# Weight halves by two GpSimd DMAs from the 21st chunk on, in a two-layer encoder on one core

## The chip, the core and the metric

One core of one Trainium2 chip. The time is device microseconds for one execution of the whole program, the median of the timed runs. The engines are TensorE (PE; PEld is its weight load), VectorE (DVE), ScalarE (ACT), GpSimd (POOL) and SyncE (SP); sixteen DMA engines move data between HBM and SBUF.

## The reference

512 tokens of 1024 channels, float32, two layers:

```
h = rmsnorm(x); q, k, v, x_rec, gate = split(h @ w_in)          # 1024 -> 2560
att = attention of 8 heads of 64 in a window of 8 x 16 on a 64-wide grid, with a learned bias
rec = (forward + backward gated linear recurrence of conv4(x_rec)) * gelu(gate)
x = x + concat(rmsnorm(att), rmsnorm(rec)) @ w_out              # 1024 -> 1024
u_act, u_lin = split(rmsnorm(x) @ w_up)                         # 1024 -> 2 x 3072
x = x + (gelu(conv3(u_act)) * u_lin) @ w_down                   # 3072 -> 1024
y = rmsnorm(x) after the second layer
```

## The kernel before

Channels lie on the partitions and the 512 tokens along the free axis. Each large product is done in three products of float32r halves (`mm3`): the weights' leading half with the activations' leading half, the leading half with the activations' rest, and the weights' rest with the leading half. A half of a weight block is 128 x 128, and a chunk is eight blocks, 128 x 1024, so that a chunk has 24 products of 512 columns. `weight_plan` lists the 205 chunks in the order in which TensorE takes them.

The weight stream has three steps. `load_to` has SyncE load chunk i into a buffer of `p_raw` (three buffers, 512 KB each). `split_to` has ScalarE copy it into a buffer of `p_hi` as float32r, which rounds it (line 173), and VectorE subtract that from the raw chunk into a buffer of `p_lo` (line 174); `p_hi` and `p_lo` have four buffers each. `chunk` hands chunk i to the products, and before that asks for splits up to chunk i + 3 and loads up to chunk i + 6.

Per layer the order is: the recurrence's input (4 chunks); a mixing stage in the order written out in `MIX` (queries, keys, recurrence gates, values and gate branch, with the heads' scores, softmax, transposes and products with the values in between); the output projection; the MLP, where `w_up` columns and VectorE's and ScalarE's work on a tile alternate, and `w_down` follows after each half of the hidden channels. The normalisations' scale 1/rms is applied to results later: TensorE sums squares over channels (`columns`), VectorE scales, GpSimd raises to the power -1/2 (line 319), and TensorE spreads the result over the partitions (`rows`, line 326). GpSimd otherwise only clears buffers: each layer's query tiles get 16 memsets (line 509).

The instructions of each engine run in the order that a scheduler wrote down when the program was built, from the program's order, priorities and buffers coming free. A buffer is taken again when all that used it is done; an instruction that needs one waits at the head of its engine's queue.

Of the kernel before, what the change touches and what calls it, by code (L numbers as in the profile page):

```python
# [14 lines left out]
P = 128  # L15
# [12 lines left out]
MASKED = -1e30  # L28
HALF = NJ // 2

# query blocks of 8 grid columns: first key column, number of key columns, offset of the bias
BLOCKS = [(0, 16, 0)] + [(8 * j - 8, 24, 128) for j in range(1, 7)] + [(48, 16, 320)]
NBIAS = 448
URGENT = 100000
# products that raise the tensor engine's clock while the first loads are under way
WARM = 9


# Order of the tensor engine's work between the recurrence's input and the output projection: tiles of
# queries, keys, values and the gate branch (whole, or halves a and b of the contraction), the recurrence's  # L40
# convolution c and gates t, scores S of a head, its transposed probabilities T and products with the values P, values
# by token u, the first steps of an output tile o.
MIX = ("q0 c0 c1 k0 t0 k1 q1 c2 t1 q2 k2 c3 t2 k3 q3 S0 v0a T0 t3 v0b g0a v1a S1 u0 P0 "
       "T1 g0b S2 v1b S3 g1a u1 T2 P1 v2a T3 P2 S4 S5 v2b g1b g2a T4 g2b P3 u2 P4 T5 S6 "
       "v3a v3b P5 g3a T6 S7 u3 o0 g3b P6 T7 o1 P7 o2 o3 o4 n o5 o6").split()
# [1 line left out]


def weight_plan():
    """128 x 128 weight blocks in the order in which the tensor engine takes them, eight a chunk."""  # L50
    plan = []
    for l in range(L):
        def pairs(w, k0, nk, ms):
            for k in range(k0, k0 + nk, 2):
                plan.append((w, l, [(k + a, m) for a in range(2) for m in ms]))

        def column(w, m):
            plan.append((w, l, [(k, m) for k in range(8)]))

        pairs("w_in", 0, 8, [12, 13, 14, 15])  # L60
        for step in MIX:
            if step in ("t0", "t0a", "t2", "t2a"):
                t = int(step[1])
                plan.append(("gate", l, [(t + a, dg) for a in range(2) for dg in range(4)]))
            elif step[0] in IN_TILE and step[-1] != "b":
                column("w_in", IN_TILE[step[0]] + int(step[1]))
        for m in range(0, 8, 2):
            plan.append(("w_out", l, [(a, m + b) for b in range(2) for a in range(4)]))
        pairs("w_out", 4, 4, [0, 1, 2, 3])
        for m in (4, 6):  # L70
            plan.append(("w_out", l, [(4 + a, m + b) for b in range(2) for a in range(4)]))
        for hf in range(2):
            j0 = hf * HALF
            for j in range(j0, j0 + HALF):
                if j == 0:
                    pairs("w_up", 0, 8, [0, NJ, 1, NJ + 1])
                elif j > 1:
                    column("w_up", j)
                    column("w_up", NJ + j)
            pairs("w_down", j0, HALF, [0, 1, 2, 3])  # L80
            seq = [(j0 + k, m) for m in range(4, 8) for k in range(HALF)]
            for i in range(0, len(seq), 8):
                plan.append(("w_down", l, seq[i:i + 8]))
    return plan
# [15 lines left out]
def encoder(ctx: ExitStack, tc: tile.TileContext, x_d, w_d, cols_d, bias_d, out_d):  # L100
# [15 lines left out]
    p_a = pool("p_a", 6)  # L116
    p_r = pool("p_r", 3)
    p_s = pool("p_s", 8)
    p_raw = pool("p_raw", 3)
    p_hi = pool("p_hi", 4)  # L120
    p_lo = pool("p_lo", 4)
    p_b = pool("p_b", 2)
    PS = bass.MemoryType.PSUM
# [19 lines left out]
    def urgent(level=2):  # L143
        return tc.high_priority(offset=level * URGENT) if level else ExitStack()

# [1 line left out]
    raws, halves = {}, {}  # L147
    state = {"load": 0, "split": 0, "use": 0}
    AHEAD_LOAD, AHEAD_SPLIT = 6, 3

# [3 lines left out]
    def load_to(n):  # L154
        while state["load"] < min(n, len(plan)):
            i = state["load"]
            raws[i] = p_raw.tile([P, 1024], F32, tag="raw", name=f"raw{i}")
            for n, sl in enumerate(pieces(i)):
                nc.sync.dma_start(raws[i][:, sl], w_d[i][:, sl])
                if i == n == 0:  # L160
                    nc.sync.dma_start(x[0], x_d[0])
            state["load"] += 1

    def split_to(n):
        while state["split"] < min(n, len(plan)):
            i = state["split"]
            load_to(i + 1)
            raw = raws.pop(i)
            hi = p_hi.tile([P, 1024], F32R, tag="hi", name=f"hi{i}")
            lo = p_lo.tile([P, 1024], F32R, tag="lo", name=f"lo{i}")  # L170
            with urgent(0):
                for sl in pieces(i):
                    nc.scalar.activation(hi[:, sl], raw[:, sl], AF.Copy)  # L173
                    nc.vector.tensor_tensor(out=lo[:, sl], in0=raw[:, sl], in1=f32(hi[:, sl]), op=ALU.subtract)  # L174
            halves[i] = (hi, lo)
            state["split"] += 1
# [15 lines left out]
        nc.tensor.matmul(ps, a[1], b[0], start=False, stop=stop)  # L192

    def gemm_group(banks, w, l, k0, nk, ms, rhs, hooks={}, first=0, total=None):
        """four tiles of the output at once, one step of the contraction after another"""
        total = total or nk
        for k in range(0, nk, 2):
            c = None
            for a in range(2):
                if k + a in hooks:  # L200
                    hooks[k + a]()
                r = rhs(k + a)
                c = c or chunk(w, l, (k0 + k, ms[0]))
                for i in range(4):
                    mm3(banks[i], blk(c, 4 * a + i), r, first + k + a == 0, first + k + a == total - 1)
# [9 lines left out]
            if k % step == step - 1:  # L215
                yield

# [1 line left out]
    cols = const.tile([P, NCOLS], F32, name="cols")  # L219
    x = []  # L220
    for k in range(ND):
# [55 lines left out]
        nc.vector.tensor_scalar(out=half_b, in0=cols[:, COLS["lru_b"]:COLS["lru_b"] + 32],  # L277
                                scalar1=0.5, scalar2=None, op0=ALU.mult)

# [1 line left out]
    def scaled_split(pl, tag, src, g, name):  # L281
        hi = big(pl, tag, name + "h", F32R)
        lo = big(pl, tag, name + "l", F32R)
# [11 lines left out]
    class Stats:  # L295
# [11 lines left out]
                nc.vector.tensor_tensor(out=self.acc, in0=self.acc, in1=sq, op=ALU.add)  # L307

        def columns(self, n, ps=None):
            """mean square + eps and its power of -1/2, token (128 s + p) at [p, s]"""  # L310
            if ps is None:
                ps = psum(ps_mm, self.name + "_cps")[:, 0:4]
            for s in range(4):
                nc.tensor.matmul(ps[:, s:s + 1], self.acc[:, s * P:(s + 1) * P], ones[:, 0:1], start=True, stop=True)
            self.ms = p_s.tile([P, 4], F32, tag="ms", name=self.name + "_ms")
            nc.vector.tensor_scalar(out=self.ms, in0=ps, scalar1=1.0 / n, scalar2=EPS,
                                    op0=ALU.mult, op1=ALU.add)
            self.r = p_s.tile([P, 4], F32, tag="rr", name=self.name + "_r")
            nc.gpsimd.tensor_tensor(out=self.r, in0=self.ms, in1=expo, op=ALU.pow)
            return self.r  # L320

        def rows(self, c, pl=ps_mm):
            """the column c of token values on every partition"""
            ps = psum(pl, self.name + "_rps")
            for s in range(4):
                nc.tensor.transpose(ps[:, s * P:(s + 1) * P], c[:, s:s + 1].to_broadcast([P, P]), ident)
# [1 line left out]
            nc.scalar.activation(r, ps, AF.Copy)  # L328
            return r

    # the token axis of the grid as columns of rows
    def by_column(ap):
        return ap.rearrange("p (c r) -> p r c", r=ROWS)

# [4 lines left out]
        return ap.rearrange("p (j h t) -> p j h t", h=2, t=64)  # L339

    class Scaled:
        """x times a norm's gain, split; the norm's 1/rms is left to the products"""

        def __init__(self, which, l):
            self.which, self.l = which, l
# [11 lines left out]
            self.st.add(x[k])  # L357

    def finish(st, down_blk, h_in, r_in, l):
        """the last two tiles of the residual and the final norm, one half of the tokens after the other"""  # L360
        N = T // 2
        sums = {}

# [53 lines left out]
        rows(1, columns(1))  # L417

    def layer(l, xn):
        # -- recurrent branch input --  # L420
        xr_ps = group_banks(1, f"xr{l}_")
        rb = None

# [28 lines left out]
            xc[t] = c  # L452
            xcs[t] = plain_split(p_h, "h", c, f"xcs{l}_{t}")

        # -- recurrences --
        fb = [None] * 4

        pair = {}
# [40 lines left out]
        qk = {}  # L499

        def query_tile(i):
            """queries of two heads, block-diagonal: (block, head, token) over the channels of both heads"""
            qk[i] = [big(p_h, "h", f"q{l}{i}{n}") for n in range(2)]

            def zones(other):
# [22 lines left out]
                nc.vector.scalar_tensor_tensor(out=by_column(qk[4 + i]), in0=by_row(ps), scalar=0.125,  # L528
                                               in1=by_row(rb), op0=ALU.mult, op1=ALU.mult)

        # -- values, token-major in key tiles of 16 columns; the tiles' second halves once more at row 0 --
        v, second = [None] * 4, [None] * 4

        def value_tile(i):
# [14 lines left out]
                nc.scalar.activation(v[i], tp, AF.Copy)  # L549
                nc.vector.tensor_copy(second[i], tp[64:P, 0:3 * P])  # L550

        # -- attention, gate branch --
        rec_stats = Stats(f"rec{l}")
        att_stats = Stats(f"att{l}")
        recs = [None] * 4
# [15 lines left out]
            rec_stats.add(fb[t])  # L571

        def finish_rec():
            # scaled so that the output's common factor is the attention's 1/rms
            f = p_s.tile([P, 4], F32, tag="f", name=f"f{l}")
            nc.vector.tensor_tensor(out=f, in0=att_stats.ms, in1=att_stats.r, op=ALU.mult)
            nc.vector.tensor_tensor(out=f, in0=f, in1=rec_stats.r, op=ALU.mult)
# [5 lines left out]
                    recs[t] = plain_split(p_xg, "xg", fb[t], f"rec{l}{t}")  # L583


        # attention step h: head pair h // 2, query blocks 0..3 or 4..7

        def scores(h):
            blocks = range(4 * (h % 2), 4 * (h % 2) + 4)
# [28 lines left out]
            return pr  # L618

        def transposes(h, pr):  # L620
            """a block's keys: a whole value tile, and half of a neighbouring one"""
            whole, part = psum(ps_pt, f"ptw{l}{h}"), psum(ps_pt, f"pth{l}{h}")
            n = 0
            for b, p in pr.items():
# [45 lines left out]
        ops, ocs, bias = {}, {}, {}  # L670

        def out_steps(m, ks):
            """steps of the contraction (attention 0..3, recurrence 4..7) of a tile of the output projection"""
            for k in ks:
                if m not in ops:
                    ops[m] = psum((ps_mm, ps_mm, ps_mm, ps_s, ps_s, ps_pt, ps_pt, ps_o)[m], f"out{l}{m}")
# [35 lines left out]
            else:  # L712
                out_steps(n, range(3))

        # -- output projection; the residual; input of the MLP --
        def add_scaled(m, ps, r, nm):
            u = big(p_t, "t", nm)
            with urgent():
# [14 lines left out]
            add_scaled(m, ops[m], ra, f"oas{l}{m}")  # L733
            xn2.ready(m)

        # -- MLP --
        rbf = [None]
        hs = {}

# [136 lines left out]
```

## Time and profile before

| | |
|---|---|
| median of 3 runs | 1235.79 us (1235.56 to 1236.59) |
| span of the profiled execution | 1234.5 us, first to last instruction |
| TensorE busy | 1217.1 us, 99% |
| VectorE busy | 764.9 us, 62% |
| ScalarE busy | 481.8 us, 39% |
| GpSimd busy | 23.7 us, 2% |
| granted clock of TensorE | 0.998 of full speed, mean |
| moved by DMA | 114 MB, mean 92 GB/s |

The profile gives no separate time for the profiled execution than its span; the timed runs lie 1.3 us above it. Busy shares are means over stages that differ. TensorE's products are drawn from their issue to a modelled end and overlap, so that short waits do not show as idle time. A wait is put down to what came last.

### The profile page before, as it was taken

How to read it: one execution, taken by the hardware profiler on the slowest of the kernel's cores; microseconds unless marked ns; L12 is line 12 of the kernel's file. 1: busy time of each engine (PE TensorE's matmuls, PEld its weight loads, DVE VectorE, ACT ScalarE, POOL GpSimd, SP SyncE). 2: the span in 40 equal slices, each digit the busy share in tenths (PEclk: the TensorE clock that was granted, in tenths of full speed). 3: DMA queues.
4: the chain of work that ended last, by engine and by line, in shares of the span. 5: the costliest groups of instructions: out<-in, count | busy, mean ns of one | idle time of the engine just before them, and what ended most of it. 6: DMA issues, size and time to landing. Idle time of an engine off the chain costs nothing.

```text
span 1234.5 us, 14411 instructions
## 1 busy us (share of the span) xinstructions
PE 1217.1 (99%) x5694; PEld 999.0 (81%) x5694; DVE 764.9 (62%) x1217; ACT 481.8 (39%) x701; POOL 23.7 (2%) x50
## 2 busy tenths in 40 slices
PE   9999999999999999999999999999999999999997
PEld 8777878888888888888887777788888888888886
DVE  7998756765544455554659977477555355555454
ACT  6676433432321232332428864344233222233220
POOL 2000000000000000000010000000000000000000
PEclk9999999999999999999999999999999999999999
DMA  7222213232332332333222221133323323323312
GB/s 259 62 86 90 76 42 103 85 103 91 97 103 94 95 102 91 97 103 96 91 85 76 76 86 52 35 122 101 99 90 103 102 87 101 102 87 102 102 52 69
DMA packets 34354, 114.07 MB, mean 92 GB/s; under 512 B 3824, under 2 KB 7024, under 8 KB 34288
## 3 DMA queue, kind: packets, MB, share of 16 engines
q1 hardware_dynamic: 34144, 113.17, 28.6%
q8 instruction: 44, 0.72, 0.2%
q14 instruction: 22, 0.18, 0.1%
q10 hardware_dynamic: 144, 0.00, 0.0%
HBM read 111.06 MB, written 2.10 MB: 92 GB/s over the span
## 4 chain that ended last, share of the span: by engine, by line
PE 93%; DVE 4%; issue 1%; DMA 0%; POOLq 0%; ACT 0%; POOL 0%; DVEq 0%; SPq 0%; ACTq 0%
PE dn L192 7%; PE dn L191 7%; PE dn L190 7%; PE pl L192 6%; PE pa L192 6%; PE pa L190 6%; PE pl L190 6%; PE pl L191 6%; PE pa L191 6%; PE out L190 2%; PE out L192 2%; PE out L191 2%; PE o L648 2%; PE o L653 2%; PE s L600 1%
## 5 line engine op out<-in xcount | busy, mean ns | idle before, releaser
L173 ACT ACTIVATE hi<-raw 128x1024 fp32r<-128x1024 f32 (+1 forms) x205 | 216.2, 1055 | 438.0 <-PE dn L191 158.9
L174 DVE TENSOR_TENSOR lo<-raw,hi 128x1024 fp32r<-128x1024 f32 (+1 forms) x205 | 249.2, 1216 | 138.0 <-ACT hi L173 137.9
L742 DVE TENSOR_TENSOR ua<-pa,g_ffn_rb 128x512 f32<-128x512 f32 x44 | 30.4, 691 | 112.8 <-PE pa L192 112.8
L750 ACT ACTIVATE uc<-uc,cols 128x512 f32<-128x512 f32 x48 | 34.8, 724 | 130.3 <-DVE uc L748 130.1
L751 DVE TENSOR_TENSOR uc<-pl,uc 128x512 f32<-128x512 f32 x44 | 30.4, 691 | 73.7 <-PE pl L192 72.0
L719 DVE TENSOR_TENSOR dns<-dn,g_ffn_rb 128x512 f32<-128x512 f32 x30 | 20.4, 688 | 29.5 <-PE dn L192 29.5
L748 DVE SCALAR_TENSOR_TENSOR uc<-ua,cols,uc 128x511 f32<-128x511 f32 x48 | 36.0, 751 | 1.6
L746 DVE SCALAR_TENSOR_TENSOR uc<-ua,cols,uc 128x511 f32<-128x511 f32 x48 | 35.8, 745 | 0.1
L612 ACT ACTIVATE p<-p,mx 128x192 f32<-128x192 f32 (+1 forms) x64 | 27.5, 431 | 16.6 <-DVE mx L610 16.6
L648 PE MATMUL o<-ptws,v 128*64 128x128 f32 x128 | 27.7, 298 | 0.0
L600 PE MATMUL s<-k,q 128*128 128x192 f32 (+1 forms) x128 | 23.0, 320 | 3.2 <-DVE q L520 2.2
L190 PE MATMUL out<-atth,hi 128*128 128x512 f32 x64 | 25.9, 405 | 0.0
L600 PEld LDWEIGHTS s<-k,q 128*128 128x128 f32 x128 | 19.9, 190 | 7.1 <-issue 4.3
L192 PE MATMUL out<-atth,lo 128*128 128x512 f32 x64 | 25.3, 395 | 0.0
L191 PE MATMUL out<-attl,hi 128*128 128x512 f32 x64 | 25.1, 392 | 0.0
L606 DVE CUSTOM_DVE_ANT_0 p<-s,bias 128x192 f32<-128x192 f32 (+1 forms) x64 | 18.3, 335 | 10.7 <-PE o L648 9.8
L745 DVE TENSOR_SCALAR uc<-ua,cols 128x512 f32<-128x512 f32 x48 | 23.4, 487 | 1.5
L520 DVE TENSOR_TENSOR q<-qps,g_mix_rb 64x256 f32<-64x256 f32 x32 | 20.6, 645 | 2.3 <-PE qps L192 1.8
L720 DVE TENSOR_TENSOR x<-x,dns 128x512 f32<-128x512 f32 x30 | 20.1, 687 | 0.4
L648 PEld LDWEIGHTS o<-ptws,v 128*64 128x64 f32 x128 | 12.2, 135 | 8.0 <-issue 3.9
L450 DVE SCALAR_TENSOR_TENSOR xc<-xrs,cols,xc 128x511 f32<-128x511 f32 (+1 forms) x24 | 17.9, 744 | 0.3
L192 PE MATMUL pl<-xg_g_ffn_4h,lo 128*128 128x512 f32 x44 | 17.1, 390 | 0.0
(918 smaller groups left out, 3475.2 us busy)
## 6 DMA issues: line engine op xcount, KB each, us to landing
raw<-in_w SPq DMA_DIRECT2D x203, 512.0 KB, 3.5
x<-in_x SPq DMA_DIRECT2D x8, 256.0 KB, 6.0
out_y<-out SPq DMA_DIRECT2D x8, 256.0 KB, 2.3
bias<-in_bias SPq DMA_DIRECT2D x8, 224.0 KB, 2.7
raw<-in_w SPq DMA_DIRECT2D x2, 256.0 KB, 3.6
cols<-in_cols SPq DMA_DIRECT2D x1, 164.0 KB, 6.7
cols<-in_cols ACTq DMA_DIRECT2D x1, 4.0 KB, 3.1
```

Source lines behind the costliest of these rows:

```text
L173: nc.scalar.activation(hi[:, sl], raw[:, sl], AF.Copy)
L174: nc.vector.tensor_tensor(out=lo[:, sl], in0=raw[:, sl], in1=f32(hi[:, sl]), op=ALU.subtract)
L190: nc.tensor.matmul(ps, a[0], b[0], start=start, stop=False)
L191: nc.tensor.matmul(ps, a[0], b[1], start=False, stop=False)
L192: nc.tensor.matmul(ps, a[1], b[0], start=False, stop=stop)
L600: nc.tensor.matmul(ps[:, o:o + ROWS * w], qt[:, b % 4 * P:(b % 4 + 1) * P], kt[:, ROWS * kc0:ROWS * (kc0 + w)], start=True, stop=True)
L648: nc.tensor.matmul(o[p0:p0 + 64, s * P:(s + 1) * P], v[i][:, s * P + p0:s * P + p0 + 64], by_head(t1)[:, 2 * (s % 2):2 * (s % 2) + 2, p0 / ...
L742: nc.vector.tensor_tensor(out=ua, in0=pa, in1=rbf[0], op=ALU.mult)
L746: nc.vector.scalar_tensor_tensor(out=c[:, 1:], in0=ua[:, :T - 1], scalar=w[0], in1=c[:, 1:], op0=ALU.mult, op1=ALU.add)
L748: nc.vector.scalar_tensor_tensor(out=c[:, :T - 1], in0=ua[:, 1:], scalar=w[2], in1=c[:, :T - 1], op0=ALU.mult, op1=ALU.add)
L750: nc.scalar.activation(c, c, AF.Gelu_apprx_tanh, bias=col("conv_ffn_b", j, l))
L751: nc.vector.tensor_tensor(out=c, in0=pl_, in1=c, op=ALU.mult)
```

## The change

From chunk `FIRST` = 20 on, `load_to` no longer loads the raw chunk by SyncE. It takes a `p_hi` buffer and has GpSimd issue a DMA from the float32 weights in HBM into that float32r buffer. `split_to` has ScalarE write minus that half into a `p_lo` buffer, and GpSimd issue a second DMA that adds the same weights from HBM to it. SyncE's load, ScalarE's rounding copy and VectorE's subtraction are gone for these 185 chunks. `p_raw` goes from three buffers to two and `p_hi` from four to five; a `p_hi` buffer is now held from the load on. `p_lo` stays at four, and the numbers of chunks asked for ahead stay. The comments that the diff takes away are left out here.

```diff
-    p_raw = pool("p_raw", 3)
-    p_hi = pool("p_hi", 4)
+    p_raw = pool("p_raw", 2)
+    p_hi = pool("p_hi", 5)
...
-    raws, halves = {}, {}
+    raws, highs, halves = {}, {}, {}
+    FIRST = 20
...
             i = state["load"]
+            if i >= FIRST:
+                highs[i] = p_hi.tile([P, 1024], F32R, tag="hi", name=f"hi{i}")
+                nc.gpsimd.dma_start(highs[i], w_d[i])
+                state["load"] += 1
+                continue
             raws[i] = p_raw.tile([P, 1024], F32, tag="raw", name=f"raw{i}")
...
             load_to(i + 1)
+            lo = p_lo.tile([P, 1024], F32R, tag="lo", name=f"lo{i}")
+            if i >= FIRST:
+                hi = highs.pop(i)
+                nc.scalar.activation(lo, f32(hi), AF.Copy, scale=-1.0)
+                nc.gpsimd.dma_start(lo, w_d[i], accum_op=ALU.add)
+                halves[i] = (hi, lo)
+                state["split"] += 1
+                continue
+            load_to(i + 1)
             raw = raws.pop(i)
             hi = p_hi.tile([P, 1024], F32R, tag="hi", name=f"hi{i}")
-            lo = p_lo.tile([P, 1024], F32R, tag="lo", name=f"lo{i}")
```

## Rows read from the trace of the kernel before

**Rows 1.** The page's head and its first part: busy us (share of the span) x instructions.
```profile
span 1234.5 us, 14411 instructions
PE 1217.1 (99%) x5694; PEld 999.0 (81%) x5694; DVE 764.9 (62%) x1217; ACT 481.8 (39%) x701; POOL 23.7 (2%) x50
```

**Rows 2.** Windows: stretch, its us, busy us (x instructions) by engine, clock, DMA share, GB/s.
```profile
60.00:120.00 60.00, 57.24 (x276) 45.62 (x275) 54.09 (x99) 45.64 (x72) 0.00 (x0) 1.00 0.28 88
...
400.00:500.00 100.00, 100.00 (x443) 82.84 (x442) 52.57 (x66) 28.00 (x32) 0.00 (x0) 1.00 0.32 100
640.00:700.00 60.00, 56.57 (x267) 45.72 (x266) 56.08 (x121) 46.60 (x84) 0.00 (x0) 1.00 0.24 78
...
1200.00:1235.00 35.00, 25.24 (x189) 23.89 (x187) 14.38 (x33) 3.26 (x6) 1.39 (x2) 0.91 0.18 61
```

**Rows 3.** Waits of TensorE from 640 to 700 us: us in total, times, longest.
```profile
PE ptw L627 <- DVE p L616: 2.3, 2, 1.5
PE s L600 <- DVE q L520: 0.7, 1, 0.7
PE s L600 <- DVE k L528: 0.5, 1, 0.5
```

**Rows 4.** Timeline of TensorE in the MLP: start, us, instruction.
```profile
400.09 0.39 PE L190 MATMUL dn<-h_9h,hi 128*128 128x512 f32 x1
```

**Rows 5.** Timeline of ScalarE in the MLP; in brackets the idle time before it.
```profile
407.55 1.06 ACT L173 ACTIVATE hi<-raw 128x1024 fp32r<-128x1024 f32 x1 [4.38 <-PE dn L191]
```

**Rows 6.** The page's costliest groups: busy us, mean ns, idle before.
```profile
L173 ACT ACTIVATE hi<-raw 128x1024 fp32r<-128x1024 f32 (+1 forms) x205 | 216.2, 1055 | 438.0 <-PE dn L191 158.9
L174 DVE TENSOR_TENSOR lo<-raw,hi 128x1024 fp32r<-128x1024 f32 (+1 forms) x205 | 249.2, 1216 | 138.0 <-ACT hi L173 137.9
```

**Rows 7.** Groups of VectorE by line and shape, 640 to 700 us.
```profile
L174 DVE TENSOR_TENSOR lo<-raw,hi 128x1024 fp32r<-128x1024 f32 x7 | 8.5, 1220 | 0.0
```

**Rows 8.** Window of the first loads.
```profile
10.00:20.00 10.00, 10.00 (x45) 8.28 (x45) 10.00 (x15) 9.59 (x14) 0.00 (x0) 1.00 0.86 299
```

**Rows 9.** DMA queues (packets, MB, share), and issues with median us to landing.
```profile
q1 hardware_dynamic: 34144, 113.17, 28.6%
...
raw<-in_w SPq DMA_DIRECT2D x203, 512.0 KB, 3.5
x<-in_x SPq DMA_DIRECT2D x8, 256.0 KB, 6.0
```

**Rows 10.** The raw loads' line alone.
```profile
DMA to landing us min/median/max: 2.9/3.5/7.1
```

**Rows 11.** Timeline of GpSimd.
```profile
186.11 1.01 POOL L319 TENSOR_TENSOR rec_r<-rec_ms,expo 128x4 f32<-128x4 f32 x1 [156.17 <-DVE rec_ms L316]
...
606.81 1.37 POOL L509 MEMSET q<- 64x256 f32 x4 [366.16 <-PE dn L191]
631.91 1.91 POOL L319 TENSOR_TENSOR g_mix_r<-g_mix_ms,expo 128x4 f32<-128x4 f32 x1 [23.72 <-DVE g_mix_ms L316]
```

**Rows 12.** Waits of ScalarE, whole span.
```profile
ACT uc L750 <- DVE uc L748: 130.1, 44, 3.1
```

**Rows 13.** Timelines of VectorE and TensorE around layer 1's first power.
```profile
631.73 1.23 DVE L174 TENSOR_TENSOR lo<-raw,hi 128x1024 fp32r<-128x1024 f32 x1
...
634.29 0.60 PE L326 MATMUL g_mix_rps<-ident,g_mix_r 128*128 128x128 f32 x4
```

**Rows 14.** Timeline of the start: VectorE's first subtractions, SyncE's last x load.
```profile
6.67 0.69 DVE L174 TENSOR_TENSOR lo<-raw,hi 128x512 fp32r<-128x512 f32 x1 [0.63 <-ACT hi L173]
...
8.78 0.33 SPq L226 DMA_DIRECT2D x<-in_x  x1
...
10.03 1.23 DVE L174 TENSOR_TENSOR lo<-raw,hi 128x1024 fp32r<-128x1024 f32 x1
```

**Rows 15.** Timelines of VectorE and TensorE: the first statistics.
```profile
19.17 0.69 DVE L307 TENSOR_TENSOR g_mix_acc<-g_mix_acc,g_mix_sq 128x512 f32<-128x512 f32 x1
...
22.52 0.94 PE L314 MATMUL cps<-ones,g_mix_acc 128*128 128x1 f32 x8
```

## What I expect, and why

> **What bounds the kernel now.** I read the page's summary first. TensorE is busy 1217.1 of 1234.5 us, VectorE 62%, ScalarE 39%, GpSimd 2% [rows 1]: only time in which TensorE stands still can be won. The windows say where that is. From 400 to 500 us, inside the MLP, it is busy 100.00 of 100 us; from 640 to 700 us, in the mixing stage of layer 1, 56.57 of 60, with VectorE at 56.08 [rows 2]. The list of waits for that stretch names VectorE's results alone, 3.5 us in four waits [rows 3]. A matmul is drawn 0.39 us long [rows 4], but in the MLP a chunk's 24 products take 4.38 + 1.06 = 5.44 us from one rounding to the next [rows 5], 0.23 each, so each listed wait hides about another 0.16: 3.5 + 4 x 0.16 = 4.1 us. That is the whole prize. Of the other 14 us that TensorE idles, the most lies in layer 0 before chunk 20 (its last value tile) and in the tail after the last chunk, as from 60 to 120 us and after 1200 us [rows 2]; the change leaves those as they are.
>
> The profiled span is 1234.5; the median of the timed runs, 1235.79, is 1.3 above it, for what lies around the span. I carry that 1.3 along and add differences to 1235.8.
>
> **What is removed.** For 185 of the 205 chunks the rounding on ScalarE (1.055 us) and the subtraction on VectorE (1.216 us) go, and a negation of the same 128x1024 shape on ScalarE comes [rows 6]. ScalarE: bounded between nothing and one more such pass per chunk, I take no change, as both are one copy of 1024 elements. VectorE is relieved of 185 x 1.216 = 225 us. In the MLP that is worth nothing, since TensorE waits for no one there. In 640 to 700 us seven subtractions, 8.5 us [rows 7], leave a VectorE that is the limit; its load falls to 47.5 of 60 us. How much of the 4.1 us that frees lies between 0 (the score, softmax and transpose chain waits for itself) and 4.1; I take two thirds, 2.8, because the waits end with VectorE's normalisation, queries and keys [rows 3], behind a queue that is idle 3.9 us in those 60, and half that relief is more than all the waits.
>
> **What is added per chunk.** Two transfers of 512 KB instead of one, both issued by GpSimd, the second reading its destination too.
>
> *DMA time.* At 299 GB/s the engines show a share of 0.86 [rows 8], so they would carry 348 GB/s and a plain 0.524 MB load takes 1.51 us of all 16. The converting load is bounded by that from below; I take it. The adding one I bound by 1.5 us (as a plain load) and 12 us (twice the 6.0 us that 256 KB of x took to land in the crowded first stage [rows 9]); I take two plain passes, 3.0 us, as it fetches weights and destination. Sum 4.5 of the 5.44 us that a chunk lasts [rows 5]: 83%, where the weight queue had 28.6% [rows 9]. It stays hidden as long as the adding transfer costs under 5.44 - 1.51 = 3.9 us, 2.6 plain loads.
> The Trainium skill, Collectives: The Full Stack, section The bandwidth ceiling, puts it that the add inside a DMA is free and the second source read is what halves the rate; by it the sum would also be two passes. No trace here shows an adding DMA yet.
>
> *GpSimd.* Two issues per chunk must fit into 5.44 us, 2.7 each. An issue on SyncE can take 0.33 us [rows 14]; GpSimd's power on 128x4 took 1.01 and 1.91 [rows 11]. I take 1.0, the nearer to an operation with little data; the ends are 0.33 and 1.91. 2.0 of 5.44: hidden.
>
> *The chain of one chunk.* With five hi buffers, the load of chunk j can be issued when TensorE is done with j-5, which leaves four chunks, 4 x 5.44 = 21.8 us, until j is due. Its negation needs the lo buffer of j-4, free 5.44 us into that; the load is there by then (1.0 to issue, 3.5 to land [rows 9]: 4.5). Then 1.06 for the negation, up to 3.1 behind a waiting ScalarE instruction (the longest wait for the gelu's input [rows 12]), 1.0 to issue, and 7 to land (two plain landings): 17.6, so 4.2 us spare. At the upper ends (1.9 for an issue, 7.1 for the landing of a load [rows 10], twice that for the add) it is 1.9 + 7.1 + 1.06 + 3.1 + 1.9 + 14.2 = 29.3: late by 7.5 us every five chunks, 1.5 a chunk.
>
> *What is queued behind it.* GpSimd takes its queue in order, and the norm's powers and the clearing of the query tiles are in it. In layer 1 the power ran at 631.91 for 1.91 us and TensorE needed it at 634.29 [rows 11, 13]: 0.5 us spare. But a subtraction ran on VectorE at 631.73 beside it [rows 13]; a power of the same size took 1.01 at 186 us with nothing beside it [rows 11]. That subtraction goes, so the spare becomes 1.4 us and one issue of 1.0 ahead of the power fits. It holds three times (two MLP norms, one mixing norm); I charge 0.5 in all. The first query memset of layer 1 waited 366 us at the head of that queue [rows 11]: harmless before. Put ahead of a load now it would stop the stream; the list shows memset and power in the order in which buffers came free, so I expect it among the loads of its own time, at no cost. The other twelve, at the first four's 1.37 us some 4.1 in a row [rows 11], hold a transfer up within its 4.2 us spare.
>
> **The first 20 chunks** keep the old path with two raw buffers. SyncE now holds chunk 2's load until chunk 0's subtraction ends at 7.36 and chunk 3's until chunk 1's ends at 11.26; x7 stands behind that, at 11.6 instead of 8.78 [rows 14]. The last sum of squares, which needs x7, ended at 19.86 and was due on TensorE at 22.52 [rows 15], so 2.7 of the 2.8 us are hidden. Between 0 and 2.8, I take 0; without that cover it would be 2.8.
>
> **Sum.** 1235.8 - 2.8 + 0.5 = 1233.5 us. This case's own range is 1230.5 to 1236.5.
>
> **Rivals.**
> *The transfers become the bound (slower).* At the adding transfer's 3.9 us the bound changes over; at three plain loads, 4.5, a chunk takes 6.0, and 185 x 0.6 = 105 us come on top: 1341. The landing chain at its upper ends would give 1.5 x 185 = 278: 1511. For it: nothing in the trace prices an adding DMA, and 83% is near. Against: the x loads' 6.0 us was queueing, and the range up to 2.6 plain loads is covered.
> *The power waits behind an accumulate that waits (slower).* The same TensorE event frees the load and the negation; if the accumulate stands ahead of the power and its hi half is late, the power starts up to 5 us late and TensorE stands 4 us, three times: 1235.8 + 12 - 1.5 = 1246. It decides where the accumulate is issued later than 1.4 us after the statistics. For it: GpSimd is in order. Against: the hi half is loaded a whole chunk earlier.
> *GpSimd and VectorE shut each other out in layer 1 (slower).* Power and subtraction side by side cost 0.9 us more than the power alone [rows 11, 13]. Were VectorE held 0.9 us by each of 16 issues from 640 to 700, it would lose 14.4 us for the 8.5 it is given, and TensorE 5.9: 1241.7. It decides at 8.5 / 16 = 0.53 us an issue.
> The Trainium skill, SBUF — State Buffer, section Who interferes with whom, has the two engines share a port that one holds to the end of its instruction, with VectorE's two-port modes and GpSimd's writes among the parties; the 1.91 beside a two-input subtraction agrees with it, while what descriptor writing does no row here shows.
> That the converting DMA passes the bits on unrounded would alter the values, not the time.
>
> **Chances.** Forecast case 0.62, transfers 0.18, power 0.12, shut-out 0.08. A run of three rounds tells about 0.2%, 2.5 us, from nothing: the limits are 1233.3 and 1238.3. The forecast case straddles the lower one: 0.32 faster, 0.29 the same, 0.01 slower. The power gives 0.04 same and 0.08 slower, the shut-out 0.03 and 0.05, the transfers 0.18 slower. Together 0.32, 0.36, 0.32. Up to 1275 the range takes in two rivals and the lowest of the third; below 1230.5 hardly anything is left.
>
> **What would show it.** Right: no subtraction after chunk 19; VectorE near 540 us busy; TensorE's waits from 640 to 700 us down to about 1.3; the DMA share near 0.8 in the MLP with TensorE at 100%; the powers near 1.0 us and no TensorE wait for the rows after them. Wrong: TensorE waits in the MLP on the adding DMA or on GpSimd's queue, a busy share of the DMA near 1, waits for g_mix_r or g_ffn_r, or VectorE's operations longer in 640 to 700 us.

## The result: 1.05% slower, and the profile after

The changed kernel takes 1250.47 us (median) where the kernel before took 1235.76 beside it. One of its four executions ran at a mean granted clock of 0.849 and took 1359.71 us; the other three give a ratio of 1.0105 to the kernel before, with a 95% interval of 1.0088 to 1.0122. I had forecast 1233.5 us, so the sign is wrong; that the time lies inside the range of 1230.5 to 1275 is luck, as its upper part stood for mechanisms that did not decide here. The profiled execution took 1249.86 us with a span of 1248.1, 13.6 above the span of before [rows 1].

The page of the changed kernel, its costliest groups (busy us, mean ns, idle before), its queues and its issues (KB each, median us to landing):

```profile
span 1248.1 us, 14546 instructions
PE 1223.2 (98%) x5694; PEld 1002.0 (80%) x5694; DVE 560.9 (45%) x1033; ACT 482.1 (39%) x701; POOL 282.0 (23%) x418
...
q0 software_dynamic: 52992, 192.96, 72.8%
q1 hardware_dynamic: 7648, 16.69, 4.1%
...
L177 ACT ACTIVATE lo<-hi 128x1024 fp32r<-128x1024 f32 x184 | 195.2, 1061 | 492.1 <-PE pa L206 158.9
L160 POOL DMA_DIRECT2D hi<-in_w x184 | 102.7, 558 | 719.5 <-PE pl L206 141.7
L178 POOL DMA_DIRECT2D lo<-in_w x184 | 159.8, 868 | 164.7 <-ACT lo L177 155.5
...
hi<-in_w POOLq DMA_DIRECT2D x184, 512.0 KB, 4.0
lo<-in_w POOLq DMA_DIRECT2D x184, 512.0 KB, 6.3
```

The change did what it says: GpSimd's queue now moves 192.96 MB, and the hardware queue that moved 113.17 [rows 9] moves 16.69; the negation costs what the rounding did, and VectorE's busy time is 204 us lower (560.9, where I had forecast near 540; the subtractions taken away add up to 224, but instructions overlap). The trace has 184 transfers of each kind, not 185: the plan has 204 chunks, and the 205 roundings of [rows 6] count the first chunk twice, as it is split in two pieces [rows 14]. An issue costs GpSimd 0.56 us for the converting load and 0.87 for the adding one.

Where the time went is read from marks that both kernels have: the first products of a norm's statistics (`cps`, `stats`, `fcps`). The chain of waits of before and then of after shows them (start, us, instruction):

```profile
184.98 0.78 PE stats L314 x8
...
237.66 0.79 PE fcps L314 x8
...
630.78 0.79 PE cps L314 x8
...
792.35 0.79 PE stats L314 x8
...
845.01 0.79 PE fcps L314 x8
...
1215.91 0.80 PE fin_cps L389 x8
```

```profile
188.51 0.80 PE stats L328 x8
...
246.00 0.79 PE fcps L328 x8
...
639.11 0.79 PE cps L328 x8
...
800.66 0.80 PE stats L328 x8
...
858.60 0.79 PE fcps L328 x8
...
1229.51 0.80 PE fin_cps L403 x8
```

From `stats` to `fcps` is the output projection, from `fcps` to the next `cps` the MLP, from `cps` to `stats` the mixing. The chain draws a mark up to 0.17 us later than TensorE's timeline does; the stages below, of all kernels in us, are differences of the timeline's marks.

| kernel | to first cps | mixing 0 | out proj. 0 | MLP 0 | mixing 1 | out proj. 1 | MLP 1 | tail |
|---|---|---|---|---|---|---|---|---|
| before | 22.52 | 162.30 | 52.68 | 393.11 | 161.57 | 52.66 | 370.90 | 18.72 |
| after | 21.97 | 166.37 | 57.49 | 393.11 | 161.55 | 57.94 | 370.90 | 18.74 |
| e1, old path everywhere, new pools | 22.21 | 164.07 | 52.65 | 393.11 | 163.16 | 52.64 | 370.90 | 18.70 |
| e2, old path for w_out | 23.08 | 166.08 | 52.65 | 393.11 | 161.45 | 52.69 | 370.90 | 18.63 |
| e3, no adding DMA | 22.38 | 163.50 | 52.67 | 393.11 | 165.10 | 52.67 | 370.90 | 18.66 |
| e4, raw 3, hi 4 | 22.19 | 162.33 | 59.56 | 457.24 | 178.10 | 57.54 | 436.45 | 18.43 |
| e5, VectorE relieved in mixing 1 | 21.67 | 162.25 | 52.67 | 393.11 | 161.47 | 52.68 | 370.90 | 18.72 |
| e6, a third load per chunk | 22.36 | 167.83 | 66.00 | 432.93 | 169.43 | 57.05 | 370.90 | 18.39 |
| e7, lo 5 | 22.14 | 164.27 | 60.78 | 452.60 | 180.64 | 59.39 | 436.72 | 18.45 |
| e8, adding DMA for w_out alone | 21.73 | 165.25 | 58.70 | 393.11 | 164.31 | 60.19 | 370.90 | 20.29 |
| e9, new path in the mixing alone | 22.94 | 163.01 | 52.65 | 393.11 | 161.38 | 52.70 | 370.91 | 18.84 |
| e10, new path in the MLP alone | 22.40 | 163.94 | 52.67 | 393.11 | 166.73 | 52.67 | 370.90 | 18.84 |

The 13.6 us are therefore +4.07 in layer 0's mixing, +4.81 and +5.28 in the two output projections, -0.55 before the first mark, and nothing in the two MLPs, in layer 1's mixing and in the tail. The list of TensorE's waits over the whole span (us, times, longest) names the new ones:

```profile
PE out L206 <- DMA lo<-in_w: 3.9, 2, 2.7
...
PE out L204 <- DMA hi<-in_w: 2.5, 2, 1.9
```

The windows of the changed kernel (columns as in [rows 2]) show the stages side by side:

```profile
113.50:120.50 7.00, 7.00 (x29) 5.17 (x28) 3.94 (x6) 1.72 (x3) 0.74 (x1) 0.51 0.16 49
...
200.00:210.00 10.00, 6.87 (x24) 4.89 (x23) 1.46 (x3) 3.12 (x4) 1.73 (x2) 0.83 0.99 227
205.70:209.10 3.40, 2.81 (x7) 2.23 (x8) 0.00 (x0) 0.00 (x0) 0.43 (x1) 0.50 1.10 255
400.00:500.00 100.00, 100.00 (x442) 82.78 (x442) 32.10 (x48) 27.41 (x31) 26.88 (x38) 1.00 0.91 193
```

In the MLP TensorE is still busy 100.00 of 100 us at a DMA share of 0.91. In the output projection (200 to 210) the share is 0.99, TensorE is busy 6.87 of 10 us and its clock averages 0.83; the kernel before had this there:

```profile
200.00:210.00 10.00, 10.00 (x46) 8.29 (x45) 5.26 (x7) 2.12 (x2) 0.00 (x0) 1.00 0.71 213
```

GpSimd's timeline of the changed kernel (in brackets its idle time and what ended it) says why the loads come late:

```profile
175.88 0.92 POOL L178 DMA_DIRECT2D lo<-in_w  x1 [0.78 <-ACT lo L177]
...
196.32 0.61 POOL L160 DMA_DIRECT2D hi<-in_w  x1 [4.37 <-PE out L206]
197.71 0.53 POOL L160 DMA_DIRECT2D hi<-in_w  x1 [0.78 <-PE out L206]
198.23 0.94 POOL L178 DMA_DIRECT2D lo<-in_w  x1
199.07 0.65 POOL L160 DMA_DIRECT2D hi<-in_w  x1
201.64 0.86 POOL L178 DMA_DIRECT2D lo<-in_w  x1 [1.92 <-ACT lo L177]
205.26 0.86 POOL L178 DMA_DIRECT2D lo<-in_w  x1 [2.76 <-ACT lo L177]
210.92 0.55 POOL L160 DMA_DIRECT2D hi<-in_w  x1 [4.80 <-PE out L206]
```

For 20 us no weight transfer is issued at all; then three loads are issued within 2.8 us, and three adding transfers follow. The first of these adds belongs to a chunk whose hi half had been loaded ahead, into the fifth hi buffer: four w_out chunks are held open, and they hold all four lo buffers. TensorE's timeline shows what that does:

```profile
203.84 0.50 PE L204 MATMUL out<-rec00h,hi 128*128 128x512 f32 x1 [1.88 <-DMA hi<-in_w]
...
206.29 0.79 PE L206 MATMUL out<-rec00h,lo 128*128 128x512 f32 x1 [1.25 <-DMA lo<-in_w]
...
207.31 0.63 PE L205 MATMUL out<-attl,hi 128*128 128x512 f32 x1
207.73 0.63 PE L206 MATMUL out<-atth,lo 128*128 128x512 f32 x1
```

A wait for hi, a wait for lo, and then products 0.43 us apart instead of 0.23: the granted clock is 0.50 from 205.7 to 209.1.

The order of TensorE's products, which the scheduler wrote, differs here too. Before, the first lo product and the twelve attention products of the last output tile come after three products:

```profile
197.25 0.50 PE L192 MATMUL out<-rec00h,lo 128*128 128x512 f32 x1
197.58 0.39 PE L190 MATMUL out<-atth,hi 128*128 128x512 f32 x1
```

After, twelve products with hi halves come first, the last four of them with the chunk that was loaded third (from 203.84), and then the lo product (206.29). So the twelve attention products, 2.7 us of work whose chunk had long been there, stand behind both waits. The timelines of e2, e3 and e10 have the order of before, that of e8 has the order of after.

### The profile page after: what moved, and what is told of

Same layout as the page of the kernel before. It is cut to its first block, busy times and chain, and to the rows that moved or that the text cites. A ratio compares the mean times of both kernels' runs of the same rounds, so it can differ in the third digit from the quotient of the medians.

```text
span 1248.1 us, 14546 instructions
## 1 busy us (share of the span) xinstructions
PE 1223.2 (98%) x5694; PEld 1002.0 (80%) x5694; DVE 560.9 (45%) x1033; ACT 482.1 (39%) x701; POOL 282.0 (23%) x418
## 3 DMA queue, kind: packets, MB, share of 16 engines
q0 software_dynamic: 52992, 192.96, 72.8%
q1 hardware_dynamic: 7648, 16.69, 4.1%
## 4 chain that ended last, share of the span: by engine, by line
PE 89%; DVE 6%; issue 2%; DMA 2%; ACT 1%; POOL 1%; POOLq 0%; DVEq 0%; ACTq 0%; SPq 0%
PE dn L205 7%; PE dn L204 7%; PE dn L206 7%; PE pl L205 6%; PE pa L205 6%; PE pl L204 6%; PE pa L206 6%; PE pa L204 6%; PE pl L206 6%; PE out L206 2%; PE o L662 2%; PE out L204 2%; PE out L205 2%; PE o L667 2%; PE s L614 1%
## 5 line engine op out<-in xcount | busy, mean ns | idle before, releaser
L177 ACT ACTIVATE lo<-hi 128x1024 fp32r<-128x1024 f32 x184 | 195.2, 1061 | 492.1 <-PE pa L206 158.9
L160 POOL DMA_DIRECT2D hi<-in_w x184 | 102.7, 558 | 719.5 <-PE pl L206 141.7
L178 POOL DMA_DIRECT2D lo<-in_w x184 | 159.8, 868 | 164.7 <-ACT lo L177 155.5
L187 ACT ACTIVATE hi<-raw 128x1024 fp32r<-128x1024 f32 (+1 forms) x21 | 21.3, 1015 | 17.5 <-DMA raw<-in_w 17.5
L188 DVE TENSOR_TENSOR lo<-raw,hi 128x1024 fp32r<-128x1024 f32 (+1 forms) x21 | 24.4, 1164 | 4.3 <-ACT hi L187 4.3
L733 DVE TENSOR_TENSOR oas<-out,att_rb 128x512 f32<-128x512 f32 x16 | 10.8, 684 | 30.5 <-PE out L206 30.5
```

The lines of the kernel that those rows point to most:

```text
L160: nc.gpsimd.dma_start(highs[i], w_d[i])
L177: nc.scalar.activation(lo, f32(hi), AF.Copy, scale=-1.0)
L178: nc.gpsimd.dma_start(lo, w_d[i], accum_op=ALU.add)
L733: nc.vector.tensor_tensor(out=u, in0=ps, in1=r, op=ALU.mult)
```

## The experiments

Theory A was that the output projections lose because their chunks are freed together. Its rivals were that the transfers are short of bandwidth throughout, and that the smaller raw pool, or GpSimd's queue in itself, costs the time.

**e1: the old path for all chunks, the new pool sizes.**
```diff
-    FIRST = 20
+    FIRST = 999
```


> The buffers of the changed kernel (two raw, five hi), but the old weight path for all 205 chunks. Theory A (of the 14.7 us, some 4 come from the smaller raw pool in layer 0's mixing stage, some 10 from the two output projections): the time from layer 0's first statistics to its second is 166.4 us as in the changed kernel against 162.3 before, the output projections take 52.7 us each as before, 1239.5 us in all. Theory B (layer 0's 4 us come from the GpSimd transfers that begin at chunk 20): 1235.8 us, layer 0 at 162.3.

Measured: 1239.24 us, 1.0030 (1.0019 to 1.0041). The two raw buffers cost 1.8 us in layer 0's mixing and 1.6 in layer 1's, and nothing in the output projections. ScalarE, from 20 to 130 us, waits for the raw loads 17.6 us in ten waits (15.0 in nine in the changed kernel), where before it was 3.0 in one, and TensorE there waits once, 1.6 us, for v.

**e2: the old path for the 16 w_out chunks** (the new condition stands in both places, in `load_to` and `split_to`).
```diff
+    def by_dma(i):
+        return i >= FIRST and plan[i][0] != "w_out"
...
-            if i >= FIRST:
+            if by_dma(i):
```


> The changed kernel, with the old path for the chunks of w_out alone (16 of the 185). Theory A (in the output projection four chunks are open at once and come free together, so that load, negation and adding transfer, some 12 us, follow one another in the open, where the old path had the raw chunk there and needed 2.3): both output projections go back to 52.7 us, TensorE shows no wait for hi or lo and no half clock there, 1240.5 us in all. Theory C (the DMA engines, at a share of 0.92, are the limit wherever TensorE has to wait): the projections keep at least half of their 4.8 and 5.3 us, 1245 us or more.

Measured: 1238.76, 1.0022 (1.0011 to 1.0032). Both output projections are back at 52.65 and 52.69. What is lost there is lost by the w_out chunks' own path.

**e3: the converting load stays, lo is made by a SyncE load and a subtraction.**
```diff
-                nc.scalar.activation(lo, f32(hi), AF.Copy, scale=-1.0)
-                nc.gpsimd.dma_start(lo, w_d[i], accum_op=ALU.add)
+                raw = p_raw.tile([P, 1024], F32, tag="raw", name=f"raw{i}")
+                nc.sync.dma_start(raw, w_d[i])
+                nc.vector.tensor_tensor(out=lo, in0=raw, in1=f32(hi), op=ALU.subtract)
```


> The converting load by GpSimd stays; the adding transfer is taken out, and the lo half comes from a plain load by SyncE and VectorE's subtraction. Theory A: the wait for the hi half's load after the release stays, that for the lo half shrinks from some 8 us to 1.2 plus the queue, so the output projections lose about 2.5 us each in place of 5, 1245 us in all; the DMA share in the MLP falls from 0.92 to about 0.56 (two plain loads, 3.0 us of 5.44). Theory C: with the share that low the projections lose nothing, 1240 us.

Measured: 1241.06, 1.0045 (1.0032 to 1.0057). The output projections lose nothing. That is what theory C forecast, and a miss for theory A in one part: I had expected the late hi loads to keep costing something. Without adding transfers beside them, and with a subtraction of 1.2 us behind them, the three late loads are in time. Full DMA engines for a few us are not the loss by themselves: here they moved 328 GB/s at a share of 0.99 from 200 to 205 us and TensorE did not wait, where in the changed kernel it was 191 GB/s at 0.89, and 263 at 1.10 in the next 5 us. Layer 1's mixing takes 3.5 us more than before in this trace, with a wait of 2.3 us for the softmax's sums and a granted clock of 0.62 from 692 to 696 us behind it; why is open.

**e8: e3, with the negation and the adding DMA back for the w_out chunks alone** (against the changed kernel; the lines behind `else` are those of e3).
```diff
-                nc.scalar.activation(lo, f32(hi), AF.Copy, scale=-1.0)
-                nc.gpsimd.dma_start(lo, w_d[i], accum_op=ALU.add)
+                if plan[i][0] == "w_out":
+                    nc.scalar.activation(lo, f32(hi), AF.Copy, scale=-1.0)
+                    nc.gpsimd.dma_start(lo, w_d[i], accum_op=ALU.add)
+                else:
...
```


> The kernel without adding transfers (plain load and subtraction instead), but with the adding transfer back for the 16 chunks of w_out. Theory A (the refill of four chunks at once in the output projection, with its adds in the open, is the loss): 3 to 5 us come back in each output projection, 55.5 to 58 us, though the DMA share elsewhere is 0.56; 1248 us in all. Theory C (the general DMA load is the loss): 52.7 us each, 1241 us in all.

Measured: 1255.85, 1.0157 (1.0143 to 1.0171). The loss is back, and more of it than the 3 to 5 us that I had expected in each projection: 6.0 and 7.5 us. TensorE's waits of this kernel (us, times, longest):

```profile
PE out L209 <- DMA hi<-in_w: 4.2, 2, 2.3
...
PE out L211 <- DMA lo<-in_w: 3.5, 2, 2.3
```

In layer 0 the two waits, 1.9 and 1.2 us, are those of the changed kernel; what is more is the half clock behind them, which lasts 6.8 us here in each projection.

With e2 and e3 this shows that the adding path of the w_out chunks (negation, adding transfer, and the order of TensorE's products that comes with them) makes the loss. A general lack of bandwidth falls: all other chunks here have no adding transfer. Theory A's mechanism, a refill in the open, is read from the timelines; no run separates it from the changed order.

**e6: a third load of every chunk, into a raw buffer that nothing reads.**
```diff
                 nc.gpsimd.dma_start(highs[i], w_d[i])
+                extra = p_raw.tile([P, 1024], F32, tag="raw", name=f"extra{i}")
+                nc.sync.dma_start(extra, w_d[i])
```


> The changed kernel plus, from chunk 20 on, a third transfer per chunk that nothing reads: a plain load of the same 512 KB by SyncE into the idle raw buffers. It measures how near the MLP is to the DMA engines' limit. Theory L (the share of 0.92 is occupancy: 5.0 of 5.44 us, so 3.5 for the adding transfer): with 1.5 more a chunk takes 6.5 us, the MLPs grow from 393.1 and 370.9 by 19%, some 77 and 72 us, 1400 us in all. Theory M (the packets' time is mostly waiting, and more fits in): the MLPs grow by under 20 us each.

Measured in two executions of it: 1305.42, 1.0559 (1.0540 to 1.0578). The first MLP grew by 39.8 us and the second by nothing, which neither theory forecast. The extra loads were held by the raw buffers alone, not by the chunks, and ran ahead: all 184 were over before the second MLP, which is untouched. In the first the engines were full:

```profile
400.00:500.00 100.00, 94.25 (x397) 73.02 (x396) 21.82 (x33) 20.71 (x22) 22.75 (x32) 1.00 1.06 316
```

A chunk took 432.93 / 393.11 x 5.44 = 5.99 us there. At 316 GB/s it moved 5.99 x 316 = 1.89 MB, 3.6 transfers of 0.524, of which 1.6 were extra. With 1.51 us for each plain load the adding transfer took 5.99 - 2.6 x 1.51 = 2.1 us of all engines, an estimate, where its landing time and the share of 0.91 suggested more. (If the share of 1.06 is what full engines show, the 348 GB/s behind the 1.51 become 369, a plain load takes 1.42 and the adding one 2.3.) So the changed kernel's first MLP had room that its share of 0.91 didn't show.

**e4: three raw buffers and four hi buffers, as before the change.**
```diff
-    p_raw = pool("p_raw", 2)
-    p_hi = pool("p_hi", 5)
+    p_raw = pool("p_raw", 3)
+    p_hi = pool("p_hi", 4)
```


> The changed kernel with the buffers of before: three raw, four hi, four lo. Theory A: layer 0's mixing goes back to 162.3 us; with no spare hi buffer no load can start before a release, so the output projections lose 6 to 8 us each in place of 5; the MLP stays hidden (0.6 + 4.0 + 1.1 + 0.9 + 6.3 = 13 of the 16.3 us that three chunks give): 1248 to 1252 us. Theory B: layer 0 keeps its 4 us, 1252 to 1256 us.

Measured: 1393.97, 1.1292 (1.1264 to 1.1319): a miss by 140 us. Layer 0's mixing is back at 162.33, as expected of the third raw buffer, but the MLPs lose 64 and 66 us, with less DMA share (0.594 of the span in its queue instead of 0.728). GpSimd's timeline of e4:

```profile
485.83 0.87 POOL L178 DMA_DIRECT2D lo<-in_w  x1 [7.58 <-ACT lo L177]
486.37 0.89 POOL L160 DMA_DIRECT2D hi<-in_w  x1
487.66 0.55 POOL L160 DMA_DIRECT2D hi<-in_w  x1 [0.41 <-PE pa L206]
494.02 0.88 POOL L178 DMA_DIRECT2D lo<-in_w  x1 [5.81 <-ACT lo L177]
495.59 0.89 POOL L178 DMA_DIRECT2D lo<-in_w  x1 [0.68 <-ACT lo L177]
```

Load and add no longer take turns. An add stands in the queue ahead of the loads and waits 5.8 to 7.6 us for its negation, and the next load, whose buffer may be free, waits with it. The power does too: TensorE waits 5.2 us in two waits for g_ffn_r in this kernel, the rival that I had named for the changed one.

**e7: five lo buffers (another pool, p_w2, gives the room).**
```diff
-    p_w2 = pool("p_w2", 2)
+    p_w2 = pool("p_w2", 1)
...
-    p_lo = pool("p_lo", 4)
+    p_lo = pool("p_lo", 5)
```


> The changed kernel with five lo buffers beside five hi buffers (the pool of the recurrence's wide tiles gives up one of its two, so the mixing stages may be slower; they are not compared). On GpSimd's queue the loads and adds no longer alternate: it reads add, add, load, add, load, load. Theory D (the queue's order sets the stream, as with three raw and four hi buffers: a load behind an add that waits for ScalarE comes late, whatever the buffers): the MLPs lose some 60 us each, as they did there. Theory E (it was the missing spare buffer): the MLPs stay at 393.1 and 370.9 us, and the output projections lose 1 to 3 us in place of 5.

Measured in two executions of it: 1394.72, 1.1281 (1.1261 to 1.1302). More buffers than the changed kernel has, and the MLPs lose as much as in e4; GpSimd's queue here runs lo, lo, hi, lo, hi, hi, and TensorE's costliest waits, 29.3 us in 20 and two groups of some 19 us, are for lo halves, not for w2.

So in e4 it was not the missing hi buffer. What the two share is the queue's order, which comes out differently with the pool sizes; that the order is the cause is read from the timelines, and no kernel with the order alone changed was run.

**e5: the kernel before, with layer 1's w_in and gate subtractions left out** (hi stands in for lo there, so that part of the computation is left out).
```diff
+            if plan[i][1] == 1 and plan[i][0] in ("w_in", "gate"):
+                nc.scalar.activation(hi, raw, AF.Copy)
+                halves[i] = (hi, hi)
...
```


> The kernel before, with one thing left out: for the 22 chunks of layer 1's input projection and gates the subtraction is dropped, and the leading half stands in for the lo half. No GpSimd transfer, no other buffers. This is VectorE's relief of the forecast by itself. Theory P1 (VectorE's queue is what TensorE waits for; the relief is worth two thirds of 4.1 us and something else in the changed kernel ate it): layer 1's mixing takes 158.8 us against 161.57, 1233 us in all. Theory P2 (the chain of scores, softmax and transposes sets those waits, and they only change their names): 161 to 162 us, 1235.5 to 1236.5 us in all.

Measured: 1235.95, 1.0000 (0.9991 to 1.0009). VectorE's busy time from 631 to 793 us falls from 128.62 to 111.69, TensorE's stays (first before, then e5):

```profile
631.00:793.00 162.00, 158.57 (x816) 125.34 (x815) 128.62 (x263) 96.79 (x174) 5.71 (x13) 1.00 0.21 68
...
631.00:793.00 162.00, 158.81 (x815) 125.51 (x815) 111.69 (x247) 96.65 (x174) 5.16 (x14) 1.00 0.20 68
```

The prize of VectorE's relief in this stage is nothing: the mixing takes 161.47 instead of 161.57.

**e9: the new path for the w_in and gate chunks alone, from the fifth chunk on.**
```diff
+    def by_dma(i):
+        return i >= 4 and plan[i][0] in ("w_in", "gate")
...
-            if i >= FIRST:
+            if by_dma(i):
```


> The new path for the w_in and gate chunks alone, from chunk 4 on in layer 0 and in all of layer 1; everything else by the old path, with two raw and five hi buffers. Theory R (VectorE's relief is worth nothing, a smaller raw pool costs only where the old path runs in the mixing): the mixing of layer 0 comes back to about 162.3 to 163 us and that of layer 1 stays at 161.5, both output projections at 52.66, both MLPs at 393.11 and 370.90: 1235 to 1237 us, no different from the kernel before. Rival (the relief of VectorE pays in layer 0 too, where it is busier): 1232 to 1234. Rival (the wait for v, which stood ahead of the half clock in the changed kernel, comes back with the two paths' changeover): mixing of layer 0 at 166, 1239 to 1241.

Measured: 1237.42, 1.0011 (1.0001 to 1.0020), 0.4 us above what I had expected at most. The mixing of layer 0 costs 163.01, that of layer 1 161.38: no gain from the relief in either layer, and no version here that beats the kernel before.

**e10: the new path for the w_up and w_down chunks alone.**
```diff
+    def by_dma(i):
+        return plan[i][0] in ("w_up", "w_down")
...
-            if i >= FIRST:
+            if by_dma(i):
```


> The new path for the w_up and w_down chunks alone; mixing and output projections by the old path with two raw and five hi buffers. Theory A (only chunks that are freed together suffer; in the MLP buffers come free one by one): both MLPs at 393.11 and 370.90, both output projections at 52.66, the mixings as with the old path and two raw buffers, 164.1 and 163.2: 1238.5 to 1240 us. Rival (the changeover back to the old path at the end of an MLP, where the first w_in chunks of layer 1 and the last chunks by the new path share buffers, holds the stream): the mixing of layer 1 above 164.5, 1241 or more.

Measured: 1241.33, 1.0045 (1.0030 to 1.0060). MLPs and output projections are exactly as before. The mixing of layer 1 takes 166.73, 3.6 more than in e1, which was the rival's figure; but the time has another place than the changeover. TensorE waits 1.1 us for v at 722.37, and the granted clock is at half from 723.9 for 6.8 us. That is the profiled execution, of 1243.51 us; two others took 1239.89 and 1239.99, inside theory A's figure.

## Why the prediction was wrong

**The chain of one chunk** is the step that failed. It lets one hi buffer come free every 5.44 us, so that four chunks of slack, 21.8 us, lie between a load and its use. That holds in the MLP. In the output projection four w_out chunks are held open together: their blocks serve the first three steps of a pair of output tiles during the mixing and the last step only after the statistics. Until then they hold four of the five hi buffers and all four lo buffers, so that one chunk's hi half is loaded ahead and no lo half. Three of them come free from 196 to 199 us, 1.4 us apart, the fourth behind the waits, at 210.9. Then three loads, three negations and three adding transfers run in the open. Not 4.2 us spare but 1.88 and 1.25 late in layer 0, 0.59 and 2.65 in layer 1, 6.4 us in all. The step asked how often a buffer comes free, not which product frees it. In the old path raw buffers are not held open, so two chunks can wait in them; that this is what saves it is argued from the pools, and what e2 shows is that its projections lose nothing: 52.65 and 52.69. How much of the 6.4 us is due to the changed order of TensorE's products stays open, since no run kept the order of before with the adding path.

**A rival that I didn't have** is the price of such a wait in clock. In each output projection, behind the waits, the clock was granted at 0.50 (1.2 of 2.4 GHz) for 3.4 us, in which products are 0.43 us apart, so half of it, 1.7 us, is lost. The sum is 6.4 of waits, 4 x 0.16 hidden in the drawing of products, and 2 x 1.7: 10.4, against 10.09 measured in the two stages. The rest of the loss is layer 0's mixing: e1's 1.8 us, and 2.3 more with 6.8 us at half clock from 113.6 us on, behind a wait of 1.4 for v:

```profile
PE o L662 <- ACT v L563: 1.4, 1, 1.4
```

The same wait, 1.2 to 1.8 us long, stands in e1, e2, e3, e8 and e10; the clock fell behind it in the changed kernel (1.4), e2 (1.2) and e8 (1.8), not in e1 (1.6), e3 (1.8) and e10 (1.6). In the timed runs it is not constant either: one execution of the changed kernel took 1245.73 us at a mean clock of 0.995, where 1249.86 and 1251.09 had 0.991. It lies 10.0 us above the median of before, about what the output projections lose alone; it has no trace, so the 1.8 and 2.3 us of layer 0's mixing are shown for the profiled execution only. What tips the clock stays open.

**The first 20 chunks** were charged nothing, with 0 to 2.8 as bounds for the start. The start was right (21.97 against 22.52 us). But the smaller pool costs 1.8 us behind it, where VectorE and ScalarE take turns with the loads; e1 shows it. I had looked only at the first x tiles.

**What is removed**: 2.8 us of gain from VectorE's relief were 0 (e5, e9, and 161.55 here). The waits that I meant to win change names, not time. From 640 to 801 us after:

```profile
PE s L614 <- DVE k L542: 1.2, 2, 0.8
...
PE ptw L641 <- DVE p L630: 0.6, 2, 0.4
```

The lower of my two ends, that the score and softmax chain waits for itself, was the true one. I took two thirds because the waits end with VectorE's operations, behind a queue that is idle only 3.9 of 60 us; a busy share is no proof that the work removed stands in the chain.

**The MLP** was right: 393.11 and 370.90 us in both kernels. The chain's terms came out at 0.56 and 0.87 us for an issue (1.0 taken), 4.0 for the load's landing (3.5) and 6.3 for the add's (7). The share was 0.91 instead of 0.83. By the share the adding transfer takes 0.91 x 5.44 - 1.51 = 3.4 us, by e6 2.1 to 2.3; I had taken 3.0. The rule of the Trainium skill that I cited (Collectives: The Full Stack, section The bandwidth ceiling), that the second source read halves the rate, is stated there for the reduce step of a collective; carried over it gives 3.0, and the two estimates lie on either side of it.

**The queue.** The power before layer 0's MLP ran in 1.03 us, with a load ahead of it at 246.08, and no TensorE wait for the rows follows in either layer; 0.5 us of the three powers was not paid:

```profile
247.07 1.03 POOL L333 TENSOR_TENSOR g_ffn_r<-g_ffn_ms,expo 128x4 f32<-128x4 f32 x1 [0.44 <-DVE g_ffn_ms L330]
```

The rivals fared thus. The transfers are no bound in steady state (MLP unchanged); in the output projections TensorE waits for transfers that were issued late, and whether the engines' rate adds to that wait is not shown. The power behind a waiting accumulate did not occur, and VectorE was not shut out: its means in layer 1's mixing are those of before. The chance that I gave to slower stood on mechanisms that did not decide here. A slip of the sums without weight: the transfers' rival adds its 105 us to 1235.8, but its 278 us to 1233.5.

## What to carry to other kernels

The slack of a prefetched buffer is not its period times the number of buffers: find the stage in which several are held and come free together, and price the whole load chain there, in the open. Look at the order in which the waiting engine takes its work: a wait also holds up what stands ready behind it. A steady stage that is hidden says nothing of that one. Before crediting an engine's relief, find the wait in the chain that it ends, or take the work away in an experiment; a busy engine beside an idle us of another isn't a cause.

## What the runs showed of the hardware

In the changed kernel an adding DMA of 512 KB lands in a median of 6.3 us and a converting one in 4.0, where the plain load before took 3.5 [rows 9]; e6's 1.06 at 316 to 318 GB/s shows that a share of 0.91 still left room. The granted clock fell to half for 3.4 or 6.8 us behind waits of 1 to 3 us in stages that were otherwise nearly full, in some traces and not in others; in the output projections that put 1.7 us on top of some 3.2 us of waits. And one lo buffer more (e7) went with a kernel 144 us slower than the changed one, in which GpSimd's queue had another order; in the changed kernel's MLP load and add take turns:

```profile
481.43 0.55 POOL L160 DMA_DIRECT2D hi<-in_w  x1 [3.26 <-PE pl L206]
482.75 0.86 POOL L178 DMA_DIRECT2D lo<-in_w  x1 [0.76 <-ACT lo L177]
486.87 0.55 POOL L160 DMA_DIRECT2D hi<-in_w  x1 [3.26 <-PE pa L206]
```
